# One more dense unit between the two maps of the widest score tile, the samples' value product earlier, and GpSimd's weight parts first

## The chip, the cores and the metric

The kernel runs on one NeuronCore of a Trainium2 chip. It is one launch: inputs lie in HBM, outputs go to HBM, and the metric is device time in microseconds (us) from start to end. Names used below: PE is the matrix engine (its weight loads are listed apart as PEld), DVE the vector engine, ACT the scalar (activation) engine, POOL the GpSimd engine, and SP the engine whose queue issues nearly all DMAs. Each engine works through its own list in order; semaphores make one wait for another.

## The reference

One inference step of a two-layer hybrid encoder, on 512 prompt frames, 16 meta tokens and 64 sample tokens, kept as 592 columns. Per layer, cut to what matters:

```python
xr, zr, q, k, v, za, g_r, g_a = in_projection(h, norm_w[l], w_in[l])   # RMSNorm, then 1024 -> 8 x 1024
q, k = rope(q, pos), rope(k, pos)
# attention, 8 heads, two maps c per head (HEAD_DIM 64, V_DIM 128)
s = einsum('bqhcd,bkhcd->bhcqk', q, k) * HEAD_DIM ** -0.5
p = softmax(where(mask, s, -inf))
attn = p[:, :, 0] - lam * p[:, :, 1]
o = einsum('bhqk,bkhe->bqhe', attn, v)
o_a = rms_norm(o, subln_w) * (1 - lam_init) * silu(za)
o_r = rglru_branch(xr, zr, ...)                                        # convolution, gates, scan
m = sigmoid(g_r) * (o_r @ w_proj_rnn) + sigmoid(g_a) * (o_a @ w_proj_att)
h = h + m @ w_out
```

Prompt frames attend within a block-causal mask (chunks of 64, meta tokens first); the 64 samples attend to 256 cached keys and themselves. All matrix products are in float32 quality.

## The kernel before

**Dense units.** Every projection is cut into blocks of 128 output channels: per layer 32 blocks for the heads (A, B, V, Z for queries, keys, values and the gate of each of 8 heads), then the gates `ga`, the recurrent branch and the projections. `dense` does one block in two halves of 296 (or 288) columns. One half is a unit: 24 matmuls into one PSUM bank `pd`, of which there are two, used in turn. For float32 quality the weights are split in a high part `wh` (ACT, L156) and a low part `wl` = weights minus `wh` (L161, on DVE, and on POOL after the units Z0, Z1 and A0 of a head). A block's weights are four k-tiles a piece, two pieces to a block: `ahead` makes the high and low parts some units before they are needed, and at the third matmul of each k-tile PE reads `wl`.

**What rides between units.** After each unit `dense` calls, in this order: `flush` (what earlier steps put off by `later`), the block's own `evac` (PSUM bank to SBUF), `step` (advances every active generator by one segment), and then the `ahead` calls for `wl` and `wh`. A head's attention is the generator `head_steps`, cut by `yield` into 26 segments. It is started after the head's unit Z1, so a segment s of head h stands behind the same unit as segment s+8 of head h-1 and s+16 of head h-2. Everything is emitted by program order: what stands ahead on an engine's list goes first.

**The segments that matter here,** as numbered before the change: 0 copies the cached keys into the tiles `ks0` and `ks1` (L447, ACT; low halves L450 and L451, DVE); 1 and 2 build the head's own keys and queries (L458 to L464); 3 and 4 compute the scores of the widest tile, query tile 3, one map each (`S_step(3, 0)`, `S_step(3, 1)`; exponentials L519); 5 to 7 the narrower tiles 2, 1 and 0, both maps at once (L510); 8 the samples' tile 4 (`S_step(4)`), which reads the cached keys in `ks0` and `ks1` again. All scores use one PSUM tile `pss` of two banks. One segment after a score tile's exponentials `combine` forms AT = P0 - lam P1 (L484 to L490); for the samples' tile it also has POOL fill the padding columns of AT with zeros (L488). Segment 10 turns the samples' AT by three PE transposes (`T_sample`, L533; the third reads the padding) and the meta part (L592). Segments 14 to 16 are the value products (PV) of tiles 3 and 2, then 1 and 0, then 4. Segment 17 is a chain of small POOL instructions on five columns, an inverse square root (L619 to L623, with L265 to L274). Segment 18 scales the output on POOL (L626, L627), 21 to 25 move it out.

`ks0`, `ks1`, `AB`, `oraw`, `PM` and `PT` have one buffer each: the next head's tile is the same memory, and its first writer waits for the last reader of the old one, wherever that reader stands in the program. `Z`, `ss` have two buffers.

Of the kernel before, what the change touches and what calls it, by code (L numbers as in the profile page):

```python
# [42 lines left out]
POOL_LO = {("Z", 0), ("Z", 1), ("A", 0)}  # L43
# [44 lines left out]
def tile_kernel(ctx, tc, I, O):  # L88
    nc = tc.nc
    V, S, P, PE, SY = nc.vector, nc.scalar, nc.gpsimd, nc.tensor, nc.sync  # L90
# [12 lines left out]
    def blk(name, dt=FT, w=T):  # L103

        return ar.tile([128, w], dt, name=name, tag="blk", bufs=ARENA)
# [4 lines left out]
    def ps_t():  # L110
        return ps.tile([128, 512], FT, name="pt", bufs=3)

    def ps_s():
        return ps.tile([128, 2, 512], FT, name="pss")

    def ps_o():
        return ps.tile([128, 512], FT, name="po")
# [47 lines left out]
    def later(f):  # L165

        deferred.append(f)

    def flush():
        fs = deferred[:]  # L170
        deferred.clear()
        for f in fs:
            f()
# [7 lines left out]
    def step():  # L181
        for g in list(active):
            try:
                next(g)
            except StopIteration:
                active.remove(g)
# [3 lines left out]
    def ahead(f, last, *x):  # L190

        for i in range(upto[f], last + 1):
            f(i, *x)
        upto[f] = max(upto[f], last + 1)

    def dense(key, xs, evac, cols, hook=None, banks=(ps_d, ps_d)):

        n = index[key]
        single = len(cols) == 1
        ahead(wdma, n + 3 + single)  # L200
        wh, wl = wt[n]
        xh, xl = xs
        for hf, (c0, m) in enumerate(cols):
            p = banks[hf]()
            i = 0
            for k in range(KT):
                for a, b in ((wh, xh), (wh, xl), (wl, xh)):
                    PE.matmul(p[:, :m], a[:, k], b[k][:, c0:c0 + m], start=(i == 0), stop=(i == 23))  # L208
                    i += 1
            flush()  # L210
            if hook:
                hook(hf)
            evac(hf, c0, m, p)
            step()
            if single:
                ahead(whi, 2 * n + 5)
            ahead(wlo, 2 * n + (5 if single else hf + 3), P if (key[1][0], hf) in POOL_LO and key[1][1] != "0" else V)
            ahead(whi, 2 * n + (6 if single else hf + 4))
        del wt[n]

# [216 lines left out]
    def head_steps(l, h, at, shared, QF, KF, kcv, vT, gate, oa):  # L437
# [36 lines left out]
        def scores(p, slot, c, q0, nq, k0, n, mask):  # L474

            nn = max(n, 256)
            PE.matmul(p[:nq, slot, :nn], qs[c][:, q0:q0 + nq], ks[c][:, k0:k0 + nn], start=True, stop=False)  # L477
            if mask == "S":
                PE.matmul(p[:nq, slot, :n], msk[:, :80], msk[:, 80:80 + n], start=False, stop=False)
            PE.matmul(p[:nq, slot, :nn], qlz[c][:, q0:q0 + nq], ks[c][:, k0:k0 + nn], start=False, stop=True)  # L480

        def combine(i, nq, n):
            rz = at.tile([128, 1], FT, name="rz", bufs=2)
            V.reciprocal(rz[:nq], Z[:nq, 1, i:i + 1])  # L484
            V.scalar_tensor_tensor(rz[:nq], rz[:nq], neg_lam(l)[:nq], Z[:nq, 0, i:i + 1], op0=OP.mult, op1=OP.mult)
            AT[i] = blk("AT")
            if i == 4:
                P.memset(AT[i][:, n:384], 0.0)  # L488
            p0, p1 = pcs[i, 0], pcs[i, 1]
            V.scalar_tensor_tensor(AT[i][:nq, :n], p1[:nq, :n], rz[:nq], p0[:nq, :n], op0=OP.mult, op1=OP.add)  # L490
            if i < 4:
                later(lambda: S.activation(AM[:, i, :NM], AT[i][:, :NM], AF.Copy))

        def S_step(i, c=None):

            if i < 4:
                q0, nq, k0, n, mask = 80 + 128 * i, 128, PAST + 64, 16 + 128 * (i + 1), "F"
            else:
                q0, nq, k0, n, mask = 0, 80, 0, n_keys, "S" if l == 0 else None
            p = ps_s()  # L500
            nm = at.tile([128, 2], FT, name="nm", bufs=2)
            if c is None:
                for cc in range(2):
                    scores(p, cc, cc, q0, nq, k0, n, mask)
                if mask == "F":
                    V.memset(p[:64, :, n - 64:n], MASKED)
                V.tensor_reduce(nm[:nq], p[:nq, :, :n], axis=AX.X, op=OP.max, negate=True)  # L507
                for cc in range(2):
                    pcs[i, cc] = blk("P")
                    S.activation(pcs[i, cc][:nq, :n], p[:nq, cc, :n], AF.Exp, bias=nm[:nq, cc:cc + 1],  # L510
                                 accum_out=Z[:nq, cc, i:i + 1])
                later(lambda: combine(i, nq, n))
            else:
                scores(p, 0, c, q0, nq, k0, 264, None)
                scores(p, 1, c, q0, nq, k0 + 264, 264, None)
                V.memset(p[:64, 1, 200:264], MASKED)
                V.tensor_reduce(nm[:, :1], p[:, :, :264], axis=AX.XY, op=OP.max, negate=True)
                pcs[i, c] = blk("P")
                S.activation(pcs[i, c][:, :528].rearrange("p (a b) -> p a b", a=2), p[:, :, :264], AF.Exp,  # L519
                             bias=nm[:, :1], accum_out=Z[:, c, i:i + 1])  # L520
                if c == 1:
                    later(lambda: combine(i, 128, 528))
# [14 lines left out]
        def PV_step(i, p):  # L537
            nq = 128 if i < 4 else 80
            if i < 4:
                j0 = i * (i + 1) // 2  # L540
                o = p[:, :128]
                PE.matmul(o, PM, vm[:, i], start=True, stop=False)  # L542
                for j in range(i + 1):
                    PE.matmul(o, PT[0][:, j0 + j], vt[:, j], start=False, stop=(j == i))  # L544
            else:
                t = PT[4]
                for j in range(2):
                    PE.matmul(p[:nq, :128], t[:, j], cv[:, j], start=(j == 0), stop=False)
                PE.matmul(p[:nq, :128], t[:, 2], vt[:, 4], start=False, stop=True)

            S.activation(oraw[:nq, i], p[:nq, :128], AF.Copy)
            sq = at.tile([128, 128], FT, name="sq")
            S.activation(sq[:nq], oraw[:nq, i], AF.Square, accum_out=ss[:nq, i:i + 1])
# [4 lines left out]
        yield  # L558
        S_step(3, 0)
        yield  # L560
        S_step(3, 1)

        kv = at.tile([128, 19, 32], FT, name="kv")
# [37 lines left out]
            SY.dma_start(PT[0][32 * g:32 * g + 32], pd.rearrange("r (j m) q t -> r j m (q t)", m=4)[:, :, g])  # L601
        yield
        yield
        yield
        oraw = at.tile([128, 5, 128], FT, name="oraw")
        P.memset(oraw[64:, 4], 0.0)
        PV_step(3, ps_o())
        PV_step(2, ps_t())
        yield
        PV_step(1, ps_o())  # L610
        PV_step(0, ps_t())
        yield
        PV_step(4, ps_t())
        rz0 = at.tile([128, 5], FT, name="rz0", bufs=2)
        V.reciprocal(rz0, Z[:, 0])
        yield
# [8 lines left out]
        on = oraw  # L625
        P.tensor_tensor(on[:, 0:4], oraw[:, 0:4], y[:, 0:4].unsqueeze(2).to_broadcast([128, 4, 128]), op=OP.mult)  # L626
        P.tensor_scalar(on[:80, 4], oraw[:80, 4], y[:80, 4:5], None, op0=OP.mult)  # L627
        yield
        yield
        yield  # L630

# [18 lines left out]
    def head(l, h, at, shared, hw, oa, hook, after):  # L650
# [46 lines left out]
        if l == 0 and h == 0:  # L697
            def rb_now(hf):
# [6 lines left out]
                else:  # L705
                    scale_rope()

            dense((l, f"V{h}"), hw, evac_v, ALL, rb_now, (ps_o, ps_t))
            for i, (c0, m) in enumerate(ALL):
                evac_a(i, c0, m, banks[0][i])  # L710
# [28 lines left out]
        def evac_zs(hf, *x):  # L739
            evac_z(hf, *x)  # L740
            if hf == 1:
                active.append(head_steps(l, h, at, shared, QK[0], QK[1], kcv, vT, lambda: zg, oa))
# [78 lines left out]
    for l in range(DEPTH):  # L821
# [33 lines left out]
        for nm in order_rnn():  # L855
            j = int(nm[2:])
            if nm.startswith("ga"):
                def evac(hf, c0, m, p):
                    if hf == 0:
                        tga[j] = blk("tg")  # L860
                    cs = slice(c0, c0 + m)
                    V.tensor_tensor(tga[j][:, cs], p[:, :m], rb[:, cs], op=OP.mult)
                    S.activation(tga[j][:, cs], tga[j][:, cs], AF.Tanh, scale=0.5)
# [105 lines left out]
        if not last:  # L969
# [37 lines left out]
            def hook(hf, acc=acc):  # L1007
                if hf == 0:
                    yy.append(sums([acc], TILES))
# [149 lines left out]
```

## Time and profile before

| | |
|---|---|
| runs of the kernel before, median of 3 | 1346.91 us (1346.74 to 1348.45) |
| the profiled execution, own time | 1349.84 us |
| its span, first to last instruction | 1348.0 us |
| PE busy in the span | 1322.0 us (98%) |
| DVE, ACT, POOL busy | 970.9 (72%), 674.9 (50%), 381.3 us (28%) |
| mean granted PE clock | 0.994 of full speed |

PE is busy nearly all the time, so what another engine does costs nothing unless PE waits for it at some point. A busy time near 100% still hides where the rest of the span goes: that is read from the list of waits and from the timeline of PE, where a wait stands in brackets behind the instruction that ended it. PE's matmuls overlap: each takes about 0.3 us from start to end, but the next starts 0.135 us later, so the lost time at a gap is read from start to start.

### The profile page before, as it was taken

The numbers are of one execution on the slowest core, as the hardware profiler recorded it, in microseconds if no ns is written. First come the engines' busy times: TensorE is split into PE (matmuls) and PEld (weight loads), VectorE is DVE, ScalarE is ACT, GpSimd is POOL, SyncE is SP. The second block draws the span as 40 slices with busy tenths as digits, with TensorE's granted clock in tenths as the row PEclk, the third lists the DMA queues.
The fourth block names the chain that finished last, engine by engine and source line by source line (L and its number), as shares of the span: only waits on it lengthen the run. The fifth ranks groups of instructions, "written<-read, shape, count | busy, mean of one in ns | idle before, by whom it ended". The sixth has DMA issues, their size and how long they took to land. (4 is left out here: it accounts for less than half of the span.)

```text
span 1348.0 us, 26348 instructions
## 1 busy us (share of the span) xinstructions
PE 1322.0 (98%) x9778; PEld 1310.9 (97%) x9778; DVE 970.9 (72%) x2024; ACT 674.9 (50%) x1577; POOL 381.3 (28%) x744
## 2 busy tenths in 40 slices
PE   8999999999999999999999999999999999999997
PEld 7999999999999999999999999999999999999997
DVE  5899888875467886655458888888744789855566
ACT  4455555564336665423425555555641466653343
POOL 4214445442302431000212244444322134200012
PEclk8999999999999999999999999999999999999999
DMA  6457776766342222223444677767663222222254
GB/s 223 123 141 178 171 177 173 173 169 158 101 129 76 75 83 79 80 79 117 169 138 134 145 182 183 183 176 189 161 154 101 87 71 87 83 80 79 90 180 137
DMA packets 260448, 179.06 MB, mean 133 GB/s; under 512 B 177952, under 2 KB 222624, under 8 KB 260320
## 3 DMA queue, kind: packets, MB, share of 16 engines
q1 hardware_dynamic: 260016, 176.85, 47.2%
q8 instruction: 77, 1.26, 0.4%
q14 instruction: 51, 0.42, 0.1%
q0 software_dynamic: 160, 0.52, 0.1%
q10 hardware_dynamic: 144, 0.01, 0.0%
HBM read 132.37 MB, written 35.26 MB: 124 GB/s over the span
## 5 line engine op out<-in xcount | busy, mean ns | idle before, releaser
L208 PE MATMUL pd<-hwh,wl 128*128 128x296 f32 (+1 forms) x1968 | 587.2, 298 | 5.0 <-POOL wl L161 4.3
L208 PE MATMUL pd<-hwh,wh 128*128 128x296 f32 (+1 forms) x1968 | 588.5, 299 | 0.1
L208 PE MATMUL pd<-hwl,wh 128*128 128x296 f32 (+1 forms) x1968 | 586.2, 298 | 0.0
L208 PEld LDWEIGHTS pd<-hwh,wl 128*128 128x128 f32 x1968 | 370.0, 188 | 7.5 <-POOL wl L161 6.2
L208 PEld LDWEIGHTS pd<-hwh,wh 128*128 128x128 f32 x1968 | 370.4, 188 | 0.3 <-DVE xs L663 0.3
L208 PEld LDWEIGHTS pd<-hwl,wh 128*128 128x128 f32 x1968 | 370.6, 188 | 0.0
L161 DVE TENSOR_TENSOR wl<-stg,wh 128x512 fp32r<-128x512 f32 x321 | 243.2, 761 | 2.2 <-ACT wh L156 2.2
L156 ACT ACTIVATE wh<-stg 128x512 fp32r<-128x512 f32 x364 | 221.6, 621 | 2.8 <-PE pss L208 1.8
L510 ACT ACTIVATE P<-pss,nm 128x400 f32<-128x400 f32 (+4 forms) x128 | 62.6, 493 | 91.2 <-DVE nm L507 90.2
L675 POOL TENSOR_TENSOR xc<-xc,xr 128x592 f32<-128x592 f32 x32 | 48.0, 1501 | 211.9 <-DMA xr<-xs 157.7
L750 ACT ACTIVATE zg<-zt 128x296 f32<-128x296 f32 (+1 forms) x64 | 28.7, 448 | 153.6 <-DVE zt L749 137.9
L161 POOL TENSOR_TENSOR wl<-stg,wh 128x512 fp32r<-128x512 f32 x43 | 63.2, 1469 | 73.9 <-ACT wh L156 50.6
L208 PE MATMUL pd<-mh,wh 128*128 128x296 f32 (+2 forms) x256 | 77.2, 301 | 0.0
L208 PE MATMUL pd<-oah,wl 128*128 128x296 f32 (+1 forms) x256 | 76.3, 298 | 0.8 <-DVE wl L161 0.8
L208 PE MATMUL pd<-orl,wh 128*128 128x296 f32 (+1 forms) x256 | 76.2, 298 | 0.0
L208 PE MATMUL pd<-orh,wl 128*128 128x296 f32 (+1 forms) x256 | 76.2, 298 | 0.0
L208 PE MATMUL pd<-mh,wl 128*128 128x296 f32 (+2 forms) x256 | 76.2, 298 | 0.0
L208 PE MATMUL pd<-orh,wh 128*128 128x296 f32 (+1 forms) x256 | 76.1, 297 | 0.0
L208 PE MATMUL pd<-oah,wh 128*128 128x296 f32 (+1 forms) x256 | 76.1, 297 | 0.0
L208 PE MATMUL pd<-oal,wh 128*128 128x296 f32 (+1 forms) x256 | 76.0, 297 | 0.0
L208 PE MATMUL pd<-ml,wh 128*128 128x296 f32 (+2 forms) x256 | 76.0, 297 | 0.0
L477 PE MATMUL pss<-ks,qs 128*128 128x264 f32 (+2 forms) x192 | 59.7, 325 | 4.8 <-ACT P L519 4.8
(250 smaller groups left out, 2518.6 us busy)
## 6 DMA issues: line engine op xcount, KB each, us to landing
stg<-in_w_dram SPq DMA_DIRECT2D x182, 512.0 KB, 3.8
pd<-AB SPq DMA_DIRECT2D x64, 160.0 KB, 3.8
PT<-pd SPq DMA_DIRECT2D x64, 160.0 KB, 3.7
xr<-xs SPq DMA_DIRECT2D x128, 74.0 KB, 4.6
od<-ob SPq DMA_DIRECT2D x64, 80.0 KB, 3.3
kv<-kv SPq DMA_DIRECT2D x64, 76.0 KB, 2.3
out_new_k_dram<-xc SPq DMA_DIRECT2D x16, 296.0 KB, 3.4
out_new_v_dram<-vT SPq DMA_DIRECT2D x16, 296.0 KB, 3.7
```

Of the source, the lines that this page charges most:

```text
L156: S.activation(hi, src, AF.Copy)
L161: E.tensor_tensor(lo, src, f32(hi), op=OP.subtract)
L208: PE.matmul(p[:, :m], a[:, k], b[k][:, c0:c0 + m], start=(i == 0), stop=(i == 23))
L477: PE.matmul(p[:nq, slot, :nn], qs[c][:, q0:q0 + nq], ks[c][:, k0:k0 + nn], start=True, stop=False)
L510: S.activation(pcs[i, cc][:nq, :n], p[:nq, cc, :n], AF.Exp, bias=nm[:nq, cc:cc + 1], accum_out=Z[:nq, cc, i:i + 1])
L675: P.tensor_tensor(xc[x][:, :T], xc[x][:, :T], r[:, :T], op=OP.add)
L750: S.activation(zg[:, cs], zt[:, cs], AF.Tanh, scale=0.5)
```

## The change

Three edits. (1) In `dense`, where POOL makes the low part, that `ahead` call now comes ahead of `step` instead of behind it. (2) In `head_steps` a second `yield` stands between `S_step(3, 0)` and `S_step(3, 1)`. (3) The samples' value product `PV_step(4)` is done one segment ahead of the frames' instead of behind them; one `yield` ahead of the value products and one behind the output scaling are taken out.

```diff
@@ dense
             evac(hf, c0, m, p)
+            E = P if (key[1][0], hf) in POOL_LO and key[1][1] != "0" else V
+            if E is P:
+                ahead(wlo, 2 * n + (5 if single else hf + 3), P)
             step()
             if single:
                 ahead(whi, 2 * n + 5)
-            ahead(wlo, 2 * n + (5 if single else hf + 3), P if (key[1][0], hf) in POOL_LO and key[1][1] != "0" else V)
+            ahead(wlo, 2 * n + (5 if single else hf + 3))
             ahead(whi, 2 * n + (6 if single else hf + 4))
@@ head_steps
         S_step(3, 0)
         yield
+        yield
         S_step(3, 1)
@@ head_steps, value products
         yield
         yield
-        yield
         oraw = at.tile([128, 5, 128], FT, name="oraw")
         P.memset(oraw[64:, 4], 0.0)
+        PV_step(4, ps_t())
+        yield
         PV_step(3, ps_o())
         PV_step(2, ps_t())
         yield
         PV_step(1, ps_o())
         PV_step(0, ps_t())
-        yield
-        PV_step(4, ps_t())
         rz0 = at.tile([128, 5], FT, name="rz0", bufs=2)
@@ head_steps, output
-        yield
         yield
         yield
```

Counted out, everything from `S_step(3, 1)` to the samples' transposes comes one segment later (the samples' scores are segment 9, their transposes 11), the frames' value products are segments 15 and 16, the POOL chain stays at 17, and the way out starts at 20 instead of 21. A head has 25 segments.

The lists of ACT, around the samples' exponentials of head h (the rows with `80x336`) and the copies of head h+1's cached keys, in layer 0. Before (L447 copies the cached keys, L156 makes `wh`):

```order
L510 ACTIVATE P,Z<-pss,nm 80x336 [waits DMAHW2_49,DMAHW4_49,DMAHW1_49,DVE_49]
L510 ACTIVATE P,Z<-pss,nm 80x336 [waits DMAHW1_49]
L447 ACTIVATE ks_2992<-kcv 64x256
L447 ACTIVATE ks_2993<-kcv 64x256
L156 ACTIVATE wh<-stg 128x512
L492 ACTIVATE AM<-AT 128x16
L458 ACTIVATE ks_2992<-xc 64x592
```

After (the same lines are L513, L450, L156, L495 and L461):

```order
L513 ACTIVATE P,Z<-pss,nm 128x144
L450 ACTIVATE ks_2968<-kcv 64x256 [waits PE_49]
L450 ACTIVATE ks_2969<-kcv 64x256 [waits PE_49]
L156 ACTIVATE wh<-stg 128x512
L495 ACTIVATE AM<-AT 128x16
L513 ACTIVATE P,Z<-pss,nm 80x336 [waits DVE_49]
```

The copies of the next head's cached keys now stand ahead of the samples' exponentials of head h, and have a wait on PE that they did not have.

The list of POOL from the low part after unit Z1 to the output scaling, in layer 1. Before (L161 is a low part, L488 the padding of the samples' AT, L619 to L623 the chain, L470 and L471 the clearing of the next head's sums):

```order
L161 TENSOR_TENSOR wl<-stg,wh 128x512 [waits DMAHW1_49,PE_49,Activation_49]
L488 MEMSET AT 128x64
L619 TENSOR_TENSOR vv<-ss,rz_10329 128x5 [waits DVE_49,Activation_49]
...
L623 TENSOR_TENSOR ny<-ny,rz_10329 128x5 [waits Pool_49]
L470 MEMSET Z 128x10
L471 MEMSET ss 128x5
L161 TENSOR_TENSOR wl<-stg,wh 128x512 [waits Activation_49]
L626 TENSOR_TENSOR oraw<-oraw,ny 128x512 [waits Pool_49]
```

After (the padding is L491, the chain L622 to L626):

```order
L161 TENSOR_TENSOR wl<-stg,wh 128x512 [waits DMAHW7_49,PE_49,Activation_49]
L161 TENSOR_TENSOR wl<-stg,wh 128x512 [waits Activation_49]
L622 TENSOR_TENSOR vv<-ss,rz_10312 128x5 [waits DVE_49]
...
L626 TENSOR_TENSOR ny<-ny,rz_10312 128x5 [waits Pool_49]
L473 MEMSET Z 128x10
L474 MEMSET ss 128x5
L491 MEMSET AT 128x64
L629 TENSOR_TENSOR oraw<-oraw,ny 128x512 [waits Pool_49]
```

The low part made after unit A0 has gone from behind the chain to ahead of it, and the padding of the samples' AT from ahead of the chain to behind it.

The list of PE around the samples' transposes after the change, in layer 1 (L596 turns the meta part, L536 the samples' AT, L480 is the first score matmul of the next head's tile 3):

```order
L596 MATMUL pt<-ident,AM 128x128 [waits Activation_49]
L536 MATMUL pt<-ident,AT 128x80 [waits DVE_49]
L536 MATMUL pt<-ident,AT 128x80
L536 MATMUL pt<-ident,AT 128x80 [waits Pool_49]
L480 MATMUL pss<-ks_10327,qs_10329 128x264 [waits DVE_49]
```

The third transpose waits for POOL's padding, as before, but it now stands behind unit B0, with `S_step(3, 0)` of the next head right behind it.

## Rows read from the trace of the kernel before

**Rows 1.** The page's first part: busy us, share of the span, instructions.

```profile
PE 1322.0 (98%) x9778; PEld 1310.9 (97%) x9778; DVE 970.9 (72%) x2024; ACT 674.9 (50%) x1577; POOL 381.3 (28%) x744
```

**Rows 2.** Waits of PE's weight loads: us in total, times, longest.

```profile
PEld pss L477 <- ACT P L519: 8.3, 15, 1.2
PEld pd L208 <- POOL wl L161: 6.2, 8, 0.9
```

**Rows 3.** Timeline of PE, both waits in one head: start, duration, instruction.

```profile
814.64 0.29 PE L208 MATMUL pd<-hwl,wh 128*128 128x296 f32 x1
815.60 0.40 PE L208 MATMUL pd<-hwh,wl 128*128 128x296 f32 x1 [0.67 <-POOL wl L161]
...
820.69 0.30 PE L208 MATMUL pd<-hwh,wl 128*128 128x296 f32 x1
821.47 0.39 PE L477 MATMUL pss<-ks,qs 128*128 128x264 f32 x1 [0.48 <-ACT P L519]
```

**Rows 4.** Timeline of PE, samples' scores and, two units later, transposes.

```profile
805.28 0.39 PE L477 MATMUL pss<-ks,qs 128*80 128x320 f32 x1
805.51 0.31 PE L480 MATMUL pss<-ks,qlz 128*80 128x320 f32 x1
...
812.60 0.37 PE L533 MATMUL pt<-ident,AT 80*128 80x80 f32 x3
```

**Rows 5.** Timeline of ACT in the same head.

```profile
808.02 0.85 ACT L447 ACTIVATE ks<-kcv 64x256 fp32r<-64x256 f32 x2
808.89 0.63 ACT L156 ACTIVATE wh<-stg 128x512 fp32r<-128x512 f32 x1
```

**Rows 6.** Timeline of POOL in the same head, low parts, padding and chain.

```profile
803.97 1.40 POOL L161 TENSOR_TENSOR wl<-stg,wh 128x512 fp32r<-128x512 f32 x1 [2.69 <-ACT wh L156]
805.31 0.15 POOL L488 MEMSET AT<- 128x64 f32 x1
806.52 0.47 POOL L619 TENSOR_TENSOR vv<-ss,rz 128x5 f32<-128x5 f32 x1 [1.06 <-ACT sq L553]
...
813.86 1.70 POOL L161 TENSOR_TENSOR wl<-stg,wh 128x512 fp32r<-128x512 f32 x1
```

**Rows 7.** Timeline of POOL, the chain in the first and in the last such head.

```profile
112.73 0.20 POOL L619 TENSOR_TENSOR vv<-ss,rz 128x5 f32<-128x5 f32 x1 [0.35 <-ACT sq L553]
119.40 0.11 POOL L470 MEMSET Z<- 128x10 f32 x1
...
911.57 0.47 POOL L619 TENSOR_TENSOR vv<-ss,rz 128x5 f32<-128x5 f32 x1 [1.00 <-ACT sq L553]
918.74 0.10 POOL L470 MEMSET Z<- 128x10 f32 x1
```

**Rows 8.** Timeline of POOL, the last head's chain of layer 0.

```profile
352.15 0.20 POOL L619 TENSOR_TENSOR vv<-ss,rz 128x5 f32<-128x5 f32 x1 [12.51 <-ACT sq L553]
357.92 1.04 POOL L626 TENSOR_TENSOR oraw<-oraw,ny 128x512 f32<-128x512 f32 x1
```

**Rows 9.** Stretches: length, busy PE, PEld, DVE, ACT, POOL, PE clock, DMA share, GB/s.

```profile
15.00:18.30 3.30, 1.49 (x9) 1.26 (x10) 3.30 (x3) 3.30 (x8) 3.14 (x3) 1.00 1.00 384
18.50:25.20 6.70, 5.84 (x24) 5.48 (x23) 4.81 (x6) 0.79 (x2) 4.78 (x8) 0.50 0.61 206
28.80:32.10 3.30, 3.30 (x15) 3.30 (x14) 2.24 (x14) 0.00 (x0) 0.00 (x0) 0.50 0.46 159
800.00:835.00 35.00, 33.85 (x256) 33.37 (x256) 29.04 (x70) 19.86 (x59) 16.56 (x33) 1.00 0.72 176
```

**Rows 10.** Timeline of PE, a long wait and, later, matmuls at half clock.

```profile
16.55 0.54 PE L429 MATMUL pd<-hwl,wh 128*128 128x296 f32 x2 [1.64 <-DVE hwl L414]
...
29.91 0.45 PE L208 MATMUL po<-hwl,wh 128*128 128x296 f32 x1
30.16 0.45 PE L208 MATMUL po<-hwh,wl 128*128 128x296 f32 x1
```

## The prediction

> **What bounds the kernel now.** I read the busy times first: PE works 1322.0 of 1348.0 us [rows 1], so only what makes PE wait, or changes its clock, can move the time. Next the list of waits of PE's weight loads, since a load stands still for about as long as PE's next start is late. Two kinds hold nearly all that PE loses inside the heads, and they are the change's targets: the second map of score tile 3 waits for the first map's exponential, because both use the one PSUM tile (8.3 us in 15 waits), and a dense unit waits for a low part that POOL made late (6.2 us in 8) [rows 2]. The timeline of PE shows both in one head: from start to start 0.96 instead of 0.135 us at the first, 0.78 at the second [rows 3]. A head takes 35.0 us, of which PE is busy 33.85 [rows 9]. Last I read POOL's timeline for why its low part is late: it stands behind the chain of the inverse square root, and starts when that ends, at 813.86 [rows 6].
>
> **What goes.** With a unit of some 3.3 us more between the maps, a wait that cost at most 1.2 us [rows 2] is gone: -8.3 us. The low part made ahead of the chain is ready before its matmul: -6.2 us. Together -14.5 us, the most the change can bring. The moved value products cost nothing by themselves: the same matmuls and ACT copies, behind another unit. No instruction and no byte of DMA is added. On SP the key and value stores move one unit, and the AB stores come behind the first rotation load instead of ahead of it; all of that is wanted units later, so I set it to 0, at most 1 us either way. The recurrent part starts a block earlier, since a head has a segment less; PE has few waits there, and I set that to 0, with 2 us either way.
>
> **What is late next.** Two instructions change sides, and I follow them along.
>
> First, ACT. The samples' scores now come after the next head has started. Its cached-key copies go into the memory that those scores still read, so ACT waits for PE to run the samples' scores, a whole dense unit later; the order shows this new wait. Behind the two copies on ACT stands the high part of weights that POOL's low part after unit A0 needs. Counted from the start of the samples' scores on PE: the first map's matmuls are through at 0.54 us [rows 4]; the two copies and the high part take 0.87 and 0.63 [rows 5], so the high part is there at 2.04.
>
> Second, POOL. That low part now stands ahead of the chain, so POOL idles until 2.04 and holds the chain up, which could have run. The low part takes 1.40 us [rows 6], to 3.44. Chain and the two clearings behind it: 7.34 us in this head (806.52 to 813.86) [rows 6]; over the ten heads that have this pattern, five to a layer, the chain runs from 6.67 us in the first to 7.17 in the last, with a mean of 7.1 [rows 7], so 7.2 with the clearings. That makes 10.64. Only then comes the padding of the samples' AT, 0.15 us [rows 6]: 10.8.
>
> PE wants that padding at the third transpose. Before, the transposes start 7.32 us after the samples' scores [rows 4], with two units between; after the change there are two units between them again, so the third is due at about 7.4. PE waits 10.8 - 7.4 = 3.4 us, with the restart 3.5. It did not wait before, because the padding then stood ahead of the chain, at 805.31 [rows 6], over 7 us early. Everything behind it on PE, the next head's scores and all further units, waits along. Ten heads make +35 us.
>
> The chain's length is the widest unknown. With DVE nearly idle it took 5.77 us (352.15 to 357.92) [rows 8]; with it PE's wait would be about 2.1 us. I take 7.2, because DVE is busy 29.04 of 35.00 us here [rows 9], as in the ten heads. The Trainium skill (SBUF — State Buffer, section "Who interferes with whom") says that DVE instructions with two SBUF inputs and POOL instructions that read SBUF exclude each other for a whole instruction. By it the chain nears 5.8 us if DVE is held up by ACT at that time, and stays at 7.2 if it is not; the ten chains against the lone one agree with the rule, and the sum would be 14 us lower by the first.
>
> In each layer two more heads have the late copies but not the late padding: one has no chain from the head before last, one no POOL low part. There ACT and DVE run some 2 us later, and I estimate 0.5 us of wait on PE in each (0 to 1.5): +2.
>
> **The clock.** In the first microseconds PE stood idle 1.64 us in one wait [rows 10] and was busy 1.49 of 3.30 us, and its granted clock fell from 1.00 to 0.50, 2.4 to 1.2 GHz, for the 6.7 us from 18.5 on; a later low stretch was 3.3 us long [rows 9]. At the low level one matmul of 296 columns follows the other after 0.25 us (29.91 to 30.16) [rows 10] instead of 0.135, so 3.3 us at it cost about 1.5, and 6.7 cost 3.1. A wait of 3.4 us is twice that one, and the shorter waits now in the heads leave the clock at 1.00 [rows 9]. I take 1.3 us for each of the ten, a little under the short stretch since some may pass without: +13; the bounds are 0 and 31.
>
> The Trainium skill (TensorE: Matmul & The Clock Gate, section "What's actually happening") says "the default state is throttled, and activity releases the throttle"; by it a wait is paid twice, once itself and once in slow matmuls behind it, and the trace's fall at 18.5 us agrees. Without such falls the sum is 13 us lower, which is a rival below.
>
> **Sum.** 35 + 13 + 2 - 14.5 = +35.5 us on the profiled execution's 1349.8, so 1385.3. That execution stands 2.9 us above the median of the runs, so the forecast for the runs is 1346.9 + 35.5, about 1382 us.
>
> **Rivals.**
> 1. PE waits for the padding, but keeps its clock. For it: half clock is seen only at the start, where DMA and DVE were at their fullest and PE's rhythm was another. Against: the idle time is longer than the one that did it. 35 + 2 - 14.5 = +22.5: 1369 us. With the short chain of 5.8 us besides, +8.5: 1355 us.
> 2. Faster: the padding is in time. Place: POOL's list between unit A0's low part and the third transpose. It decides at 3.4 us: if the chain with what stands ahead of it ends that much sooner, all of the 14.5 us are kept but for small waits of about 2. For it: POOL is busy only 16.56 of 35 us [rows 9]. Against: its idle time lies ahead of the low part, where it waits for ACT, and the chain is a row of dependent instructions that does not shrink. 1346.9 - 12 = 1335 us.
> 3. Nothing to be measured: the padding is nearly in time, and late PSUM evacuations behind the held-up ACT and DVE eat the gain. ACT has to do the samples' exponentials and the copies of own keys and queries behind the same unit now. About 1 us in 14 heads against 14.5: 1347 us.
> 4. The change does not do what it says, and the second map still waits. That would need the first map's exponential to be over 3 us later, which only PE's own stop would bring, and that moves both; folded into the others.
>
> **How the numbers follow.** Forecast (padding late, clock falls) 0.60; rival 1 0.21; rival 2 0.11; rival 3 0.08. The forecast's own range is 1363 (chain near 5.8 us, falls at some) to 1400 (clock low for 6.7 us each time: 35 + 31 + 2 - 14.5 = +53.5). The range that should hold the time is 1353 to 1402: it leaves out rivals 2 and 3 and a little of the upper end. What a measurement of this kernel can tell from no change is about 0.2%, 2.7 us. Slower by more than that: 0.60 + 0.21 and a fourth of rival 3, 0.83; within it 0.06; faster 0.11.
>
> **What would show it.** In the profile after: the waits for the exponential L522 and for POOL's L161 are gone from PE's list, and in their place stands a wait of the transposes L536 for the padding L491, ten times about 3.4 us, and in the timeline POOL's chain begins about 3.4 us after the samples' scores do. ACT shows a stop of some 2 us ahead of L450, ended by PE. The clock's row dips under 1.0 in both stretches of heads, where it is 1.00 now. Wrong I am if the transposes run without a wait, for then the kernel gets faster; if the waits are there and the clock stays at 1.00, rival 1 is right.

## The result and the profile after

The changed kernel takes 1414.34 us (median of 4 runs, 1412.13 to 1415.45) against 1347.68 us before (4 runs beside it): ratio 1.0489, 95% interval 1.0469 to 1.0509. The direction is as forecast, the size is not: 66.7 us slower, where 35.5 were forecast, and outside the range (1353 to 1402). The profiled execution spans 1410.3 us against 1348.0, so 62.3 us are to be found in it.

The busy times of the page, which answer to [rows 1]: PE has the same 9778 matmuls, but is busy 95% of the span instead of 98%, and 17 us longer in all.

```profile
PE 1339.4 (95%) x9778; PEld 1327.5 (94%) x9778; DVE 958.6 (68%) x2024; ACT 673.8 (48%) x1577; POOL 378.4 (27%) x744
```

The waits of PE's weight loads (total, times, longest), which answer to [rows 2]; "issue" stands for a wait that the profile puts down to nothing it shows:

```profile
PEld pt L536 <- POOL AT L491: 37.3, 10, 3.9
PEld pss L480 <- ACT P L513: 17.9, 13, 4.6
PEld pd L432 <- DVE hwl L417: 6.0, 6, 1.9
PEld pt L596 <- ACT AM L495: 3.7, 7, 1.1
PEld po L547 <- issue: 1.5, 2, 1.2
```

Both waits that the change aimed at are gone (8.3 and 6.2 us before). The padding wait is there, ten times. And the second row is new: PE waits 17.9 us, nearly all of it for the exponentials of score tile 2, which the prediction does not name.

The forecast wait in one head, in the timeline (start, duration, instruction), which answers to [rows 4 to 6] and shows the two clock levels of [rows 10]:

```profile
853.23 0.31 PE L480 MATMUL pss<-ks,qs 128*80 128x320 f32 x1
...
853.73 0.86 ACT L450 ACTIVATE ks<-kcv 64x256 fp32r<-64x256 f32 x2 [0.63 <-PE pss L483]
...
855.32 1.29 POOL L161 TENSOR_TENSOR wl<-stg,wh 128x512 fp32r<-128x512 f32 x1 [4.54 <-ACT wh L156]
856.56 0.21 POOL L622 TENSOR_TENSOR vv<-ss,rz 128x5 f32<-128x5 f32 x1
...
864.35 0.11 POOL L473 MEMSET Z<- 128x10 f32 x1
...
864.43 0.16 POOL L491 MEMSET AT<- 128x64 f32 x1
...
860.91 0.31 PE L536 MATMUL pt<-ident,AT 80*128 80x80 f32 x2
864.64 0.40 PE L536 MATMUL pt<-ident,AT 80*128 80x80 f32 x1 [3.42 <-POOL AT L491]
...
865.80 0.45 PE L208 MATMUL pd<-hwh,wh 128*128 128x296 f32 x1
866.04 0.45 PE L208 MATMUL pd<-hwl,wh 128*128 128x296 f32 x1
```

From the start of the samples' scores (853.23) ACT's copies hold up the high part, POOL's low part starts at 2.09, the chain starts at 3.33 and runs 7.79 us, the padding is done at 11.4, and the transposes are due at 7.7. Behind the wait the matmuls follow each other after 0.24 us: from 864.6 to 868.0 the granted clock is 0.50, which is 1.2 GHz.

Stretches (length, busy PE, PEld, DVE, ACT, POOL, granted PE clock, DMA share, GB/s), which answer to the last of [rows 9]. The matmuls of one head, 256, now need 40 us instead of 35, at a granted clock of 0.96 instead of 1.00:

```profile
845.00:885.00 40.00, 35.72 (x256) 35.13 (x256) 28.04 (x70) 19.65 (x61) 15.91 (x32) 0.96 0.60 155
```

The trace's clock records show 12 low stretches, besides one in the last microseconds that the kernel before has too. Ten follow the padding waits (seven of 3.4 us, three of 6.8, together 44.4 us), two follow long waits for tile 2's exponentials (10.2 us together). In the kernel before there are two, 10.2 us, both in the first 40 us; the profile after has none there. A low microsecond loses 0.45 us (0.135 against 0.247 us from matmul to matmul), so the clock costs 20.0 us behind the padding, 4.6 behind tile 2, and 4.6 less at the start.

The sum for the profiled execution: padding 37.3, tile 2's scores 17.9, meta columns and value products (rows 4 and 5 of the list) 5.2, clock 20.0, all other rows of the list together about 0, less 14.5 for the two waits that went: 65.9, of 62.3 measured (the list counts the loads, whose stops are a little longer than the matmuls').

Where the new row comes from is in the timeline of one head: SP's queue, POOL, ACT and PE.

```profile
781.41 4.65 SPq L600 DMA_DIRECT2D pd<-AB  x4
788.84 2.54 SPq L605 DMA_DIRECT2D PT<-pd  x4
...
792.07 2.44 SPq L672 DMA_DIRECT2D xr<-xs  x4
...
798.13 1.43 POOL L677 TENSOR_TENSOR xc<-xc,xr 128x592 f32<-128x592 f32 x1 [13.64 <-DMA xr<-xs]
799.62 0.20 POOL L609 MEMSET oraw<- 64x128 f32 x1
...
799.85 0.27 ACT L554 ACTIVATE oraw<-pt 80x128 f32<-80x128 f32 x1 [10.34 <-POOL oraw L609]
...
800.47 0.57 ACT L513 ACTIVATE P<-pss,nm 128x400 f32<-128x400 f32 x1
...
801.75 0.59 PE L480 MATMUL pss<-ks,qs 128*128 128x272 f32 x1 [4.41 <-ACT P L513]
```

Read from below: PE needs the PSUM that tile 2's exponentials read. These stand on ACT behind the copy of the samples' value product into `oraw`, which waits for POOL's clearing of `oraw`. The clearing stands on POOL behind the second rotation addition, which waits for its load. And that load stands in SP's queue behind the load of PT, which itself waits until the AB store (`pd<-AB`; this `pd` is a buffer in HBM, not the PSUM bank) has landed, to 788.84, and takes 2.54 us more to issue.

Two lists show the same over the whole kernel. SP's stops at PT's load until the AB store has landed, before and after:

```profile
SPq L601 <- DMA pd<-AB: 7.4, 6, 1.9
SPq L605 <- DMA pd<-AB: 48.8, 26, 4.4
```

And ACT's stops at the copy into `oraw` for the clearing, after; the list of before has no such row:

```profile
ACT oraw L554 <- POOL oraw L609: 80.2, 12, 10.9
```

### The profile page after: what moved, and what is told of

Its sections match the earlier page's. It is cut to its first block, busy times and chain, and to the rows that moved or that the text cites. A ratio compares the mean times of both kernels' runs of the same rounds, so it can differ in the third digit from the quotient of the medians.

```text
span 1410.3 us, 26286 instructions
## 1 busy us (share of the span) xinstructions
PE 1339.4 (95%) x9778; PEld 1327.5 (94%) x9778; DVE 958.6 (68%) x2024; ACT 673.8 (48%) x1577; POOL 378.4 (27%) x744
## 5 line engine op out<-in xcount | busy, mean ns | idle before, releaser
L208 PE MATMUL pd<-hwh,wh 128*128 128x296 f32 (+1 forms) x1968 | 595.8, 303 | 0.0
L208 PE MATMUL pd<-hwl,wh 128*128 128x296 f32 (+1 forms) x1968 | 592.7, 301 | 0.0
L208 PEld LDWEIGHTS pd<-hwl,wh 128*128 128x128 f32 x1968 | 378.8, 192 | 0.0
L208 PEld LDWEIGHTS pd<-hwh,wh 128*128 128x128 f32 x1968 | 378.2, 192 | 0.5 <-issue 0.2
L208 PEld LDWEIGHTS pd<-hwh,wl 128*128 128x128 f32 x1968 | 376.6, 191 | 1.2 <-DVE wl L161 1.2
L161 DVE TENSOR_TENSOR wl<-stg,wh 128x512 fp32r<-128x512 f32 x321 | 240.1, 751 | 2.3 <-ACT wh L156 2.2
L156 ACT ACTIVATE wh<-stg 128x512 fp32r<-128x512 f32 x364 | 220.6, 621 | 4.1 <-PE pss L208 1.8
L161 POOL TENSOR_TENSOR wl<-stg,wh 128x512 fp32r<-128x512 f32 x43 | 63.7, 1483 | 139.2 <-ACT wh L156 98.5
L513 ACT ACTIVATE P<-pss,nm 128x400 f32<-128x400 f32 (+4 forms) x128 | 62.1, 489 | 44.4 <-DVE nm L510 42.7
L480 PE MATMUL pss<-ks,qs 128*128 128x264 f32 (+2 forms) x192 | 63.5, 342 | 15.2 <-ACT P L513 15.1
```

Source lines behind the costliest of these rows:

```text
L156: S.activation(hi, src, AF.Copy)
L161: E.tensor_tensor(lo, src, f32(hi), op=OP.subtract)
```

## The experiments

Each was timed in rounds with the kernel before (1347.7 to 1347.9 us). The terms: "padding early" takes the zero fill of the samples' AT out of `combine` and puts it ahead of tile 0's scores, "clearing early" makes and clears `oraw` one segment sooner. The wait for tile 2's exponentials is listed as one for L510, L512 or L513, by the kernel's line numbers.

**The load of PT alone, one segment later (changed kernel otherwise).** This came last, but tells most directly what made tile 2 late.

```diff
         T_sample()
         yield
+        yield
         PT[0] = at.tile([128, 10, 128], FT, name="PT")
...
         yield
-        yield
         oraw = at.tile([128, 5, 128], FT, name="oraw")
```

> The changed kernel with one edit: the load of PT a segment later, so that it stands behind the second rotation load in SP's queue and not ahead of it. Theory A: the order of SP's queue is what made the clearing late; the score wait for tile 2's exponentials (17.9 us) goes to 4 or less, with its two long low-clock stretches, and the wait for the padding stays or grows a little, since PE comes to it earlier (37 to 45 us, as it does today: 10 times); the frames' products may wait for PT by some 5 to 15 us: 1398 us (1390 to 1412). Rival B: the load's place is of no account, the clearing is late for the addition itself or for PE's own stop: the score wait stays at 12 us or more and the time is 1414 us or above.

Measured 1401.88 us (1399.75 to 1403.01), ratio 1.0399 (1.0384 to 1.0415). Its PE waits, then SP and POOL at the same place of the same head:

```profile
PEld pt L536 <- POOL AT L491: 37.4, 10, 3.9
...
PEld pss L480 <- ACT P L513: 2.4, 4, 0.9
```

```profile
779.89 4.66 SPq L600 DMA_DIRECT2D pd<-AB  x4
784.65 0.79 SPq L141 DMA_DIRECT2D stg<-in_w_dram  x1
785.53 2.48 SPq L672 DMA_DIRECT2D xr<-xs  x4
788.12 2.56 SPq L606 DMA_DIRECT2D PT<-pd  x4
...
793.51 0.20 POOL L609 MEMSET oraw<- 64x128 f32 x1
```

Theory A holds. PE comes to this place 1.5 us sooner than in the changed kernel. The rotation load is issued 6.5 us sooner, so 5.0 sooner against PE's work, and the clearing stands 6.1 us sooner, so 4.6 against PE's work. PE's wait falls from 17.9 to 2.4 us, ACT's for the clearing from 80.2 to 11.9, and the padding wait stays. The span falls by 10.4 us. The parts come to 9.5: 15.5 of waits and 4.6 of the two low stretches less, 2.9 of waits at the value products more, and 7.7 more clock, since the ten low stretches now last 61.4 us instead of 44.4.

**Padding early; clearing early; both; low parts behind the chain again.** Four kernels from the changed one.

```diff
# padding early
-            AT[i] = blk("AT")
-            if i == 4:
-                P.memset(AT[i][:, n:384], 0.0)
+            if i < 4:
+                AT[i] = blk("AT")
...
+        AT[4] = blk("AT")
+        P.memset(AT[4][:, n_keys:384], 0.0)
         S_step(0)
# clearing early
         yield
-        yield
         oraw = at.tile([128, 5, 128], FT, name="oraw")
         P.memset(oraw[64:, 4], 0.0)
+        yield
         PV_step(4, ps_t())
# low parts behind: edit (1) of the change undone
```

> The changed kernel (1414.3 us), with the samples' AT and its padding set up one segment earlier, so that POOL clears the padding ahead of the low part and of the chain. Theory A (the ten waits of the third transpose are a matter of POOL's order, and each pulls the clock down): the 37.3 us of waits for the padding go, and with them ten of the twelve low stretches of the clock, some 20 us; the waits of the score matmul L480 for exponentials, 17.9 us, stay. About 1414 - 57 = 1357 us (1350 to 1365). Rival B (the stop only moves: ACT and DVE run late behind the copies of the cached keys, and PE stops at the next transpose or at an evacuated bank instead): no lower than 1380 us, with as much wait at L596 or at the dense units. Rival C (the waits matter, the clock's falls do not): 1414 - 37 = 1377 us.

> The changed kernel with the clearing of the output tile oraw one segment earlier, ahead of POOL's rotation add that waits for a DMA. Theory A (the samples' value product now stands first, its copy on ACT waits for that clearing, the clearing stands on POOL behind an add that waits for a DMA, and tile 2's exponentials stand on ACT behind the copy): the waits of L480 for L513 fall from 17.9 to under 2 us, and the two low stretches of the clock that follow the two long ones go, 4.6 us. About 1414 - 21 = 1393 us (1388 to 1398); the padding's 37 us stay. Rival B (the exponentials are late because ACT has too much to do): no change, 1410 us or more.

> Both of the former together: the changed kernel with padding and clearing early. Theory A: both kinds of new waits gone, what is left is the 14.5 us that the change saves against some 4 to 8 us of small waits for the meta part's copy and for evacuated banks behind the late copies of the cached keys: 1337 to 1346 us, a little under the kernel before. Rival B (the late key copies by themselves cost as much as the change saves): 1347 to 1355 us.

> The changed kernel without its first edit: POOL's low parts behind the step again, as before. The chain then need not wait for the late high part; worked out from the rows of before it ends some 4.7 us after the samples' scores start, the low part some 1.5 us later, and the padding at about 6.4, ahead of the third transpose at 7.4. Theory A (the long padding wait needs two things together, POOL's low part ahead of the chain and the high part held up behind the key copies): no padding wait over 0.5 us, ten low stretches of the clock gone; L480's 17.9 us stay, POOL's low part may cost 0.5 us in some heads. About 1360 us (1352 to 1368). Rival B (the padding is late because the samples' scores come a segment later, whatever POOL does first): waits of 2 us or more at the third transpose stay, 1385 us or more.

Measured: padding early 1431.36 us, ratio 1.0613 (1.0595 to 1.0631); clearing early 1394.05, 1.0337 (1.0321 to 1.0352); both 1375.12, 1.0200 (1.0177 to 1.0223); low parts behind 1434.24, 1.0636 (1.0618 to 1.0653). The first and the last were expected far faster and came out slower than the change itself. PE's waits with padding early:

```profile
PEld pss L480 <- ACT P L512: 61.8, 16, 5.6
```

and with low parts behind:

```profile
PEld pss L477 <- ACT P L510: 64.8, 16, 6.0
```

In both the padding wait has left the list, as expected of each. But PE's stop at the padding, 3.7 us, had given SP and POOL that time in each of ten heads. Without it the clearing is later still against PE: ACT's stops for it grow from 80.2 us to 127.7 with padding early, 12 times in either. The wait for tile 2 grows to more than padding and tile 2 had cost together. The changed kernel shows the same within itself: its two long waits for tile 2, 4.4 and 4.6 us, come ahead of the first padding stop of each layer, and behind such a stop none is over 1.8 us. The 17.9 us is thus only what the first wait left uncovered of the second. With clearing early, theory A's number (1393) came out:

```profile
PEld pt L536 <- POOL AT L491: 37.4, 10, 3.9
...
PEld pss L480 <- ACT P L513: 2.9, 5, 0.9
```

Both early was expected a little under the kernel before, and was 27 us over it. The timeline there shows a third thing late, DVE's gate product, which waits for a load that stands behind others in SP's queue; tile 0's maxima stand behind it on DVE:

```profile
223.56 0.83 DVE L651 SCALAR_TENSOR_TENSOR oa<-oa,lm,zg 128x592 f32<-128x592 f32 x1 [3.72 <-DMA oa<-od]
...
226.15 0.57 PE L480 MATMUL pss<-ks,qs 128*80 128x336 f32 x1 [3.38 <-ACT P L512]
```

**Padding early and PT's load later.** The edits of both, as above.

> The kernel with the padding early (1431.4 us), and PT loaded one segment later, so that on SP's list the second rotation load stands ahead of PT and no longer behind PT's wait for the AB stores. In the kernel with the padding early, PE waits 61.8 us at L480 in 16 waits. Theory A (SP's list is the cause: the change put the AB stores right ahead of PT, SP stands still 3 us a head until they land, the rotation load and with it POOL's add, the clearing, the copy of the samples' product and tile 2's exponentials are late by that and by PT's own issue): L480's waits fall to under 12 us, most low stretches of the clock go, up to 1 us a head comes back at the value products that wait for PT. About 1355 us (1345 to 1367). Rival B (the rotation load is late for another reason, the key block's evacuation on DVE): L480's waits stay over 35 us, 1390 us or more.

Measured 1389.03 us, ratio 1.0298 (1.0271 to 1.0325): a miss. The wait for tile 2 fell from 61.8 to 2.4 us, but without the padding stop PT itself comes too late for the frames' products, as the list of PE's matmuls shows:

```profile
PE po L546 <- DMA PT<-pd: 30.0, 10, 4.2
```

**Both early, and the unit behind the output scaling back; and with PT's load later besides.**

```diff
         P.tensor_scalar(on[:80, 4], oraw[:80, 4], y[:80, 4:5], None, op0=OP.mult)
         yield
+        yield
         yield
```

> The kernel with padding and clearing early (1375.1 us), with the yield behind the output scaling put back, so that the way out (od, oa and the product with the gate on DVE) is as far behind as in the kernel before. Theory A (what is left there, 26.9 us at L480, is DVE standing at the gate product for the oa load, with tile 0's maximum and exponentials behind it): L480's waits fall under 6 us, the four low stretches of the clock go, about 1375 - 21 - 7 = 1347 us (1341 to 1352). Rival B (tile 0's exponentials are late because ACT is held up by the copies of the next head's cached keys): L480's waits stay over 20 us, 1370 us or more.

> Padding and clearing early, PT's load and the way out one segment later each. Theory A (after those four nothing new is late but the small waits behind the key copies: meta copy 3.5, low parts on DVE 6.4 us): about the kernel before, 1343 us (1337 to 1349). Rival B (a later PT makes the value products wait 1 us or more in each head): 1355 us or more.

Measured 1362.81 us, ratio 1.0114 (1.0092 to 1.0135), and 1365.99, 1.0134 (1.0111 to 1.0157). With the unit back tile 2 and tile 0 are in time (26.9 to 5.1 us), as theory A expected of the gate product's load, and no low stretch is left in the first. But both are slower than before, against the expectation, and PT's load later, the only difference between them, gains nothing: the wait for tile 2 and tile 0 falls from 5.1 to 2.5 us, that for PT's landing grows from 1.0 to 5.6. In the first a fourth wait stands in their place, for ACT's copies of the meta columns (3.5 us with both early):

```profile
PEld pt L597 <- ACT AM L494: 15.4, 13, 1.6
PEld pd L208 <- DVE wl L161: 6.5, 9, 1.3
```

**Key copies a segment later,** once with clearing early, once with all of the above but PT's load.

```diff
+        yield
         AM, qlz, vt, vm = shared
...
         later(cache_lows)
-        yield
```

> The changed kernel with the clearing early, and the next head's cached keys copied one segment later, behind the samples' scores, so that ACT no longer waits for PE there; the padding stays behind the chain on POOL. Theory A (the long wait for the padding comes half from the key copies: without them the high part and POOL's low part are some 3 us earlier, and so are chain and padding): the padding's waits fall from 37.4 us (3.7 each) to under 12 us; what then comes up is the 25 us of DVE's wait for oa, as in the kernel with both early. 1365 to 1385 us. Rival B (the chain's place alone makes the padding late): waits of 3 us or more each stay, 1394 us.

> The changed kernel with padding and clearing early and the unit behind the output scaling back (1362.8 us), and the key copies a unit later besides. Theory A: what was left there, the 15.4 us of waits for the copy of the metas, comes from ACT's stop at the key copies, so it falls to 3 to 4 us as in the kernel without early copies, and the rest stays: about 1350 us (1346 to 1354). Rival B: that wait is made by DVE being late; it stays at 10 us or more: 1360 us or more.

Measured 1373.46 us, ratio 1.0189 (1.0170 to 1.0208), and 1358.40, 1.0076 (1.0055 to 1.0098). In the first the padding wait falls from 37.4 to 12.2 us: ACT's stop at the key copies, which holds up POOL's low part, makes two thirds of it. The rest is gone in the kernels above that move the padding or the low part:

```profile
PEld pss L480 <- ACT P L513: 17.1, 12, 3.6
PEld pt L536 <- POOL AT L491: 12.2, 8, 2.6
```

The second falls between the two theories (1346 to 1354, and 1360 or more). The wait for the metas goes from 15.4 to 8.0 us and no further, so ACT's stop is half of its cause; the other half stays open.

**Each edit alone on the kernel before.** Low parts first: edit (1) only. Values first: edit (3) with a `yield` behind the frames' products, so that heads keep their length. Unit between: edit (2) only, with the samples' product in the segment of the last frames' one, so that the way out does not move. And low parts and values first together.

> The kernel before with the first part of the change alone (POOL's low parts ahead of the chain). Theory A: this part is harmless and useful as long as the key copies stand behind the samples' scores: POOL's wait of PE goes (6.2 us in 8 waits), the padding still stands ahead of the chain, nothing new waits: 1341 us, about 0.4% faster. Rival B: holding up the chain moves the output scaling and all behind it, as in the changed kernel: 1350 us or more, with a new wait in PE's list.

> The kernel before with the order of the value products alone (the samples' before the frames'; heads keep their length). The clearing then stands ahead of the second rotation addition on POOL, as the order shows, and so does not wait for that addition's load. Theory A: the moved products cost nothing by themselves; the cost came with the segment more, which put the clearing behind an addition whose load waits in SP's queue: 1347 us (1344 to 1350). Rival B: the samples' copy ahead of tile 2's exponentials is late by itself: 1 to 2.5 us in each of 14 heads, 1362 to 1382 us, with a score wait of 15 us or more in PE's list.

> The kernel before with the unit between both maps alone; the value products keep their order, and the samples' go into the segment of the last frames' ones to win back the segment. Theory A: the wait for the first map's exponential (8.3 us) goes, the low parts' wait (6.2) stays, the padding is in time since the chain runs without the low part ahead of it, the clearing is wanted a segment later than in the changed kernel; the copy of the metas gets late behind the held-up ACT (up to 12 us): 1340 to 1352 us. Rival B: the extra segment alone brings the clearing's chain (addition, load, SP's queue) onto the path: a score wait of 15 us or more, 1365 us or more.

> The kernel before with the low parts ahead and the samples' value product first, without the unit between the maps; heads keep their length. Theory A: each of the two is as good beside the other as alone (6.5 and 3.8 us less), and the whole loss hangs on the unit and the segment that the heads lose to it: 1337.5 us (1335 to 1341), no wait for the padding. Rival B: the two hurt each other (the low part's chain is late for the samples' products): 1345 us or more.

| edit on the kernel before | us | ratio, 95% |
|---|---|---|
| low parts first | 1341.44 | 0.9948 (0.9932 to 0.9965) |
| values first | 1344.15 | 0.9969 (0.9956 to 0.9981) |
| both of these | 1343.40 | 0.9970 (0.9960 to 0.9981) |
| unit between | 1379.62 | 1.0232 (1.0206 to 1.0257) |

Low parts first is the fastest of all, 0.5% under the kernel before, as expected. Its list of PE's waits, and that of values first:

```profile
PEld pss L480 <- ACT P L522: 8.8, 14, 1.2
PEld pd L432 <- DVE hwl L417: 5.7, 5, 1.9
```

```profile
PEld pss L477 <- ACT P L519: 9.6, 11, 1.5
PEld pd L429 <- DVE hwl L414: 5.5, 6, 1.9
```

POOL's low part, 6.2 us before [rows 2], is gone from both: each edit alone removes the same wait. Why values first removes it was not looked into. With one wait to remove, the two together have nothing to add up, where theory A expected 1337.5. For the first, the profile has no low stretch at the start, where before and the other two have 10.2 us (4.6 us of time). Among executions of one mean granted clock, 0.998, the median is 1346.4 us before (17), 1342.8 with values first (4) and 1342.8 with both (3), and low parts first has 1340.4 and 1342.1: about 5 of its 6.5 us stay.

Unit between fell outside theory A (1340 to 1352): it loses 32 us by itself, on rival B's side, but at another place than B said.

```profile
PE po L544 <- DMA PT<-pd: 11.5, 10, 2.5
PE pt L593 <- ACT AM L492: 5.0, 12, 0.8
...
PE pss L477 <- ACT P L510: 4.1, 8, 0.7
```

The wait for the first map is gone there too. But PT is late for the frames' products, and small waits for ACT and DVE come beside it. SP's stops at PT's load are there already, as long as in the changed kernel, while each of the other three has 8.5 to 8.7 us of them:

```profile
SPq L602 <- DMA pd<-AB: 51.6, 26, 4.2
```

So the unit alone brings the new order of SP's queue. The kernel also has the samples' product in the segment of the last frames' one, and no run tells the two apart; PT's wait stands ahead of that product.

## Why the prediction was right in direction and wrong in size

**What goes: right.** Both waits left the list, 14.5 us.

**The padding wait: right.** Ten times 3.5 was forecast, 37.3 us in ten was measured, and three kernels show its cause: it is gone with the padding early and with the low parts behind, and falls by two thirds with the key copies later. Its parts in the head shown: low part 2.09 us behind the scores (2.04 forecast), then 1.29 (1.40), the chain 7.79 (7.1; 7.8 to 7.9 in all ten), the transposes due at 7.7 (7.4). The lone chain took 5.77 [rows 8]; here DVE was busy 6.89 of 7.90 us. Only ACT's stop ahead of the key copies was shorter than the 2 us named as a sign: 0.63 us here, 2.0 at most.

**The clock: right in kind, too small.** 1.3 us each was forecast, 13 in all. Every one of the ten waits brought a low stretch, 20.0 us together; less 4.6 at the start, which no edit explains, and with the 4.6 of the other waits. "Since some may pass without" was wrong in this kernel, and this term was 7 us too small. The Trainium skill (TensorE: Matmul & The Clock Gate, section "What's actually happening") has the throttled state as the default that activity releases; these ten waits, each with a stretch at 0.50 behind it, agree with it.

**The step that failed** is the one on SP's queue: "all of that is wanted units later, so I set it to 0, at most 1 us either way", and with it "the moved value products cost nothing by themselves". The second sentence is true on the old grid (values first alone is 3.8 us faster, not slower). Together with the extra unit it is not: SP's stops for the AB store grew from 7.4 to 48.8 us, and the order of its queue cost 17.9 us of PE's waits and 4.6 of clock, 22.5 of the 27 us that the sum missed in the profiled execution; moving PT's load alone took the wait from 17.9 to 2.4 us. Of the time it gave back 10.4 us, mostly because the clock then stayed low for longer behind the padding waits; clearing early gave back 18.7. What was left of the 27 us is the 7 of the clock, 3.2 of small waits and 2.3 of the padding, less the 4.6 at the start and 3.6 that the list counts too much. The prediction looked at what SP's transfers are wanted for (AB's way through HBM, the stores) and not at what stands behind them in the same queue: the second rotation load, and through POOL and ACT, in order, tile 2's exponentials. The trace of before had a sign of it that I did not follow: POOL's clearing of `oraw`, behind the same addition, came at 833.05, 3.8 us behind the end of PE's work of that unit (829.29), with two more units until it was wanted; the change took these away.

```profile
829.29 0.38 PE L542 MATMUL po<-vm,PM 128*128 128x128 f32 x2
...
833.05 0.20 POOL L606 MEMSET oraw<- 64x128 f32 x1
```

**The rest.** +2 for small waits was 5.2. Of the rivals, the first (clock kept, 1369) is refuted by the clock, the second (padding in time, 1335) by the ten waits; had the padding been in time the time would have been 1431, not 1335, as padding early shows. The third (1347) is refuted by the time, the fourth by the list, in which the wait for the first map is gone. The rivals took each wait as if the next one were not waiting behind it.

What stays open: the best kernel with the unit (1358.4) is still 10 us over the kernel before, and 15 over the one with low parts and values first and no unit. The metas' copies hold 8.0 us of waits in it, of which only ACT's part is understood.

## What to carry to other kernels

When an edit moves a DMA in a queue that issues in order, price what stands behind it there, not only what it loads, and follow that through every engine to PE. A wait on the engine that bounds the kernel gives all others time: before counting its removal as gain, subtract it from the slack of the next late thing, head by head. Two edits that each remove a wait may remove the same one; their gains are read from the list of waits, not added.

## What was not expected of the hardware

A DMA in SP's queue whose source has not landed held all behind it: PT's load stood from 786.06 to 788.84 for the landing of the AB store, and the rotation load went out 5.0 us later against PE's work than with PT behind it. And the same ten waits of 3.6 to 3.9 us gave low-clock stretches of 44.4 us in one kernel and 61.4 in another, each stretch 3.4 or 6.8 us long.
